# A hybrid decoder layer on one core: ten pairs begun ahead instead of six and eight, HGRN results one head later

## The chip, the cores and the metric

The kernel runs on one core of a Trainium2 chip. The time is the device time of one execution, in microseconds (us); the figure compared is the median of several executions. Engines are called by the profile's names: PE (TensorE's matmuls) and PEld (its weight loads), DVE (VectorE), ACT (ScalarE), POOL (GpSimd) and SP (SyncE, which here only issues transfers; all loads and stores stand in its one queue, in program order).

## The reference

One post-norm decoder layer in f32, on 1024 tokens of width 1024, cut here to what is computed:

```python
z = h @ W_in                      # cut into HGRN q, f, i, g; SWA q, k, v; memory q; three gates
o_a = hgrn2(q, f, i, lb)          # 8 heads, state 128x128, chunks of 64:
                                  #   S_t = diag(f_t) S_{t-1} + (1-f_t) v_t^T ;  o_t = S_t^T q_t
o_a = o_a * rsqrt(mean(o_a^2)) * hg_norm_gain * silu(g)
o_b = sliding_window_attention(...)  # 16 heads, window 128, T5 bias, sinks
o_c = memory_attention(...)          # 4 heads, 256 memory rows
merged = sum_b sigmoid(gate_b) * (o_b @ W_branch_b)
h = layer_norm(alpha * h + merged @ W_out)
h = layer_norm(alpha * h + relu(h @ W_up)^2 @ W_down)
```

## The kernel before, in words

Every f32 operand is held as a rounded high part and the rest (`split`: ACT writes the high part, DVE or POOL subtracts it to get the low part), and a product takes three matmuls: high by high, high by low, low by high. The six large products (gates with the HGRN output gate, three branch products, up, down) are also done by a two-by-two scheme with seven block products instead of eight. The scheme needs sums of quarters of the weights (line 301, on DVE, in place in the raw tile `R`) and of the operand (`combine`). A block product `prod` is twelve matmuls of 128x512.

One *run* makes four 128x512 results from two raw weight tiles: products 1 and 2 need the plain weights `w1` and the left operand `x` (tile `X`); products 3 to 7 need weight sums (`w2`, `w3`, `w4`) and operand sums `xs[3]` to `xs[7]`, which live in tiles `O`, `O`, `T`, `MG`, `BT`. `prepare` loads and sums a run's weights, `run` does the products. Products 1 and 2 of a run need no sums, so some runs begin ahead with a *pair* (`two`, 24 matmuls): the first product is copied to a tile, stored to memory, and read back at the run itself, which then is shorter ("held" below). The pairs stand where the operand sums are still being made:

- Gate stage: six pairs (`EARLY_Z`), and after each of the first four one `x_rest(k)`: two raw tiles of x are loaded, four sums made in place on DVE, five operands split (DVE, ACT, POOL). Then 16 runs.
- Up stage: eight pairs (`EARLY`, in `first_two`), and after each of the first four a deferred `flip_h1(1, n, ...)`: eight transposes of 128x128 on PE, ACT copies, the same sums. Then 16 runs.
- Branch stage: three branches in the order 1, 2, 0, each with three pairs and four runs. After each product result `b_emit` adds the snapshot of another product, multiplies with the gate (`th`, read from memory) and adds to the merged sum. The snapshot sits in a `G` tile, the value `v` goes into the second half of an `S` tile, and the merged sum, where it comes from memory, into a `G` tile.

The HGRN heads run per half of the tokens (`hf`), head by head: `z_q` (query product), `mid` (transposed keys `kt`, masked scores `at`, new state), `outp` (output, its squares, the scaled output `os`), `last` (transposes `os`, multiplies with the output gate `sg`, stores). `kt` and `os` are the halves of one `S` tile. The w_out stage holds eight weight tiles; each result row block does two halves `f` of 24 matmuls over `k`, half 0 first.

A scheduler keeps each engine's program order as written and lets tiles of a name go round in a fixed number of buffers: X 2, O 2, MG 2, BT 2, T 4, W 4, R 4, S 2, G 4; PSUM banks z 3, s 3, t 2. A new tile waits until the one that many turns before it is read for the last time; a load waits in SP's queue, and what stands behind it waits too.

Of the kernel before, what the change touches and what calls it, by code (L numbers as in the profile page):

```python
# [15 lines left out]
P = 128  # L16
# [3 lines left out]
TH = 512  # L20
# [7 lines left out]
NFF = 4096 // 256  # L28
EARLY = 8
EARLY_Z = 6  # L30
EARLY_B = 3
# [5 lines left out]
def hybrid_layer(ctx: ExitStack, tc: tile.TileContext, a: dict, out: bass.AP):  # L37
# [370 lines left out]

    for i in range(EARLY_Z):
        two(zsrc(i)[0], z_keep(i), z_first(i))  # L410
        if i < 4:
            x_rest(i)
    for i in range(16):
# [3 lines left out]
    def zload(br, m, hf):  # L417
        t = st("G", [P, TH])
        nc.sync.dma_start(t, d_z[4 * br + m // 2, 2 * hf + m % 2])
        return t  # L420
# [85 lines left out]
    def swa_phase(hf, x, one, fill_last):  # L506
# [46 lines left out]
        for tp in range(4):  # L553
            if tp < 3:
                qn = st("T", [P, 2, 2, TH], F32R)
                fill = [lambda: z_sq(qn, tp + 1, 0), lambda: one(2 * tp), lambda: z_sq(qn, tp + 1, 1),
                        lambda: one(2 * tp + 1)]
            else:
                fill = [lambda: one(6), lambda: one(7)] + fill_last
            for n in range(4):  # L560
                u = 4 * tp + n
                box = units[u - 1][4] if n % 2 else []
                sc, fl, pv = swa_unit(hf, tp, n, q, kk, bt, pxa[:, n % 2], box)
                units.append((tp, n, fl, pv, box))
                sc()
                fill[n]()
                if u:
                    units[u - 1][2]()
                if u > 1:
                    finish_unit(u - 2)  # L570
            if tp < 3:
                q = qn
# [88 lines left out]
    def hg_head(hf, h, fk, gg, el, x, v, wk):  # L661
# [5 lines left out]
        box = {}  # L667
# [8 lines left out]
        def mid():  # L676
            two_ = st("S", [P, 2, TH])
            kt, box["os"] = two_[:, 0], two_[:, 1]
            box["sg"] = zload(3, h, hf)
            ko = pt("t")  # L680
# [4 lines left out]
            for n in range(4):  # L685
                cs = slice(n * P, (n + 1) * P)
                mm(ao[:, cs], km[:, cs], qm[:, cs], True, True)
            nc.vector.copy_predicated(at, causal.bitcast(I32).unsqueeze(1).broadcast_to([P, 4, P]),
                                      ao.rearrange("p (n c) -> p n c", n=4))
            ko = pt("s")  # L690
            for n in range(4):
# [15 lines left out]
        def outp():  # L707
            osv = box["os"].rearrange("p (n d) -> p n d", d=P)
            oo = pt("s")
            for n in range(4):  # L710
# [19 lines left out]

        return z_q, mid, outp, last

# [16 lines left out]
    for hf in range(NH):  # L749
# [38 lines left out]
        heads = []  # L788
# [10 lines left out]
        for h in range(8):  # L799
            if h == 2:  # L800
                vs.append(st("T", [P, 2, 4, 256]))
                ggs.append(hgs[1][3]())
            if h < 7:
                head(h + 1)
            if h:
                heads[h - 1][2]()
            if h % 2 == 0 and h < 6:
                g = h // 2 + 1
                zv(vs[g // 2][:, g % 2], g)
            heads[h][1]()  # L810
            if h:
                heads[h - 1][3]()
            if hf:
# [12 lines left out]
        if hf == 0:  # L826
            x = nx
        heads[7][2]()
        heads[7][3]()

    accs = {}
# [22 lines left out]
    def b_emit(e, i):  # L854
        br = order[e]

        def emit(b, o, s_):
            t = st("S", [P, 2, TH])
            th, v = t[:, 0], t[:, 1]
            nc.sync.dma_start(th, d_z[4 * br + i, b])  # L860
            home = accs.get((i, b))
            if home is None and e:
                mg = st("G", [P, TH])
                nc.sync.dma_start(mg, d_mg[slot[i, b]])
# [60 lines left out]
    wo = []  # L925
    for i, tag in enumerate(("W", "MG", "MG", "BT", "BT", "W", "T", "T")):
        t = st(tag, [P, 2, 1024], F32R)
        load_here(t[:, 0:1, :], t[:, 1:2, :], a["w_o"][(i % 2) * 4 + i // 2].unsqueeze(1), lo_engine())
        wo.append(t)
    wo = [wo[0::2], wo[1::2]]  # L930
    xv = a["x"].rearrange("(b p) d -> p b d", p=P)
# [80 lines left out]

    for i in range(EARLY):
        first_two(i)
        if i < 4:
            deferred.pop(0)()
# [319 lines left out]
```

## Time and profile before

| | before |
|---|---|
| median of 3 runs | 2241.71 us (2240.56 to 2247.29) |
| profiled execution | 2244.91 us |
| its span in the trace | 2242.9 us |
| PE busy | 2067.9 us, 92% of the span |
| DVE busy | 1415.4 us, 63% |
| ACT busy | 890.2 us, 40% |
| POOL busy | 941.3 us, 42% |
| mean granted TensorE clock | 0.963 of full |

The span is what the trace covers, the profiled execution's time has 2.0 us around it. PE is busy nearly throughout; what it loses is 175 us of the span and some time at a lower granted clock. The stages in order of time: memory keys and values to 56 us; gate stage 56 to 395 (its pairs to 110); window attention and memory heads for the first half of the tokens, HGRN heads 654 to 760; the same for the second half, HGRN heads 1023 to 1145; branches 1132 to 1443; w_out and the first layer norm 1444 to 1549; up pairs 1549 to 1623 and up runs to 1889; down and the last layer norm to 2243.

### The profile page before, as it was taken

Reading aid. Unit: us, or ns where it says so; the run is one execution under the profiler, and the core shown is the slowest. Engines: PE = TensorE matmul, PEld = TensorE weight load, DVE = VectorE, ACT = ScalarE, POOL = GpSimd, SP = SyncE. Lnnn points to the kernel's source line nnn. Section 1 sums busy time; section 2 is a strip of 40 time slices with the busy share of each in tenths; the row PEclk is TensorE's granted clock in tenths of the full one; section 3 lists DMA queues with packets and bytes.
Section 4 is the critical chain, followed back from the end, with each engine's and each line's share of the span. In section 5 each row is a group of like instructions: output and inputs, shape, how many; then the busy total and the mean of one; then the engine's idle time right before and its main releaser. Section 6 shows DMA issues by size and latency. Waiting matters only on the chain.

```text
span 2242.9 us, 27033 instructions
## 1 busy us (share of the span) xinstructions
PE 2067.9 (92%) x9906; PEld 1684.5 (75%) x9906; DVE 1415.4 (63%) x2206; ACT 890.2 (40%) x1558; POOL 941.3 (42%) x430
## 2 busy tenths in 40 slices
PE   8799999999999999999978797898899999999987
PEld 8577888777788777778866575677678887788865
DVE  5643335676554577576475777846566555688898
ACT  4423433444443344363332333413534555433321
POOL 1533333211222222523256454634523334777774
PEclk9899999999999999999999898999899999999998
DMA  8544324322333323554356646434656445744322
GB/s 283 188 154 124 110 97 135 108 86 76 104 118 132 99 95 108 193 202 168 105 191 236 210 151 198 145 112 165 197 186 212 155 155 202 286 154 156 113 85 75
DMA packets 150901, 340.22 MB, mean 152 GB/s; under 512 B 13376, under 2 KB 30960, under 8 KB 150768
## 3 DMA queue, kind: packets, MB, share of 16 engines
q1 hardware_dynamic: 150160, 336.37, 45.1%
q10 hardware_dynamic: 608, 2.11, 0.2%
q8 instruction: 78, 1.28, 0.2%
q14 instruction: 55, 0.45, 0.1%
HBM read 248.76 MB, written 89.67 MB: 151 GB/s over the span
## 4 chain that ended last, share of the span: by engine, by line
PE 33%; DVE 10%; POOL 8%; issue 6%; DMA 6%; ACT 3%; SPq 0%; POOLq 0%; DVEq 0%; ACTq 0%
PE pz L62 16%; PE ps L62 10%; PE pt L62 7%; POOL W L78 3%; DVE S L301 1%; POOL MG L78 1%; DMA R<-d_o 1%; DVE S L870 1%; DVE T L301 1%; DVE R L301 1%; ACT W L77 1%; DMA S<-d_z 1%; POOL BT L78 1%; DMA R<-in_w_up_dram 1%; ACT S L475 1%
## 5 line engine op out<-in xcount | busy, mean ns | idle before, releaser
L78 POOL TENSOR_TENSOR W<-R,W 128x1024 fp32r<-128x1024 f32 x200 | 495.4, 2478 | 959.5 <-ACT W L77 924.8
L77 ACT CAST W<-R 128x1024 fp32r<-128x1024 f32 (+1 forms) x289 | 283.6, 982 | 389.1 <-DVE R L301 168.4
L62 PE MATMUL pz<-X,W 128*128 128x512 f32 x1344 | 342.9, 407 | 33.2 <-POOL W L78 18.1
L62 PEld LDWEIGHTS pz<-X,W 128*128 128x128 f32 x1344 | 256.9, 195 | 95.6 <-POOL W L78 23.9
L62 PE MATMUL pt<-O,W 128*128 128x512 f32 x1056 | 275.3, 410 | 37.8 <-DVE S L301 23.1
L62 PEld LDWEIGHTS pt<-O,W 128*128 128x128 f32 x1056 | 205.3, 197 | 95.4 <-DVE S L301 27.4
L301 DVE TENSOR_TENSOR R<-R,R 128x512 f32<-128x512 f32 x132 | 99.4, 756 | 162.8 <-POOL W L78 138.2
L62 PE MATMUL pz<-O,W 128*128 128x512 f32 x816 | 200.4, 399 | 0.7 <-POOL W L78 0.7
L62 PEld LDWEIGHTS pz<-O,W 128*128 128x128 f32 x816 | 151.7, 190 | 33.3 <-POOL W L78 1.1
L62 PE MATMUL pz<-MG,W 128*128 128x512 f32 x528 | 133.1, 399 | 7.8 <-ACT W L77 7.6
L62 PE MATMUL pz<-BT,W 128*128 128x512 f32 x528 | 131.6, 399 | 8.2 <-DVE G L301 8.2
L62 PE MATMUL ps<-X,W 128*128 128x512 f32 x528 | 131.3, 397 | 0.0
L62 PE MATMUL ps<-T,W 128*128 128x512 f32 x528 | 128.3, 390 | 0.3 <-ACT T L77 0.3
L62 PEld LDWEIGHTS pz<-BT,W 128*128 128x128 f32 x528 | 100.4, 192 | 33.6 <-ACT W L77 8.6
L62 PEld LDWEIGHTS pz<-MG,W 128*128 128x128 f32 x528 | 101.6, 193 | 31.7 <-ACT W L77 9.2
L62 PEld LDWEIGHTS ps<-X,W 128*128 128x128 f32 x528 | 102.1, 194 | 22.1
L62 PEld LDWEIGHTS ps<-T,W 128*128 128x128 f32 x528 | 99.3, 188 | 21.6 <-ACT T L77 0.8
L78 DVE TENSOR_TENSOR W<-R,W 128x512 fp32r<-128x512 f32 (+1 forms) x91 | 92.7, 1019 | 29.2 <-ACT W L77 28.3
L78 POOL TENSOR_TENSOR MG<-R,MG 128x1024 fp32r<-128x1024 f32 (+1 forms) x39 | 100.6, 2580 | 17.7 <-ACT MG L77 16.1
L78 POOL TENSOR_TENSOR BT<-R,BT 128x1024 fp32r<-128x1024 f32 x31 | 84.9, 2740 | 52.8 <-ACT BT L77 52.8
L297 ACT COPY G<-pz 128x512 f32<-128x512 f32 x104 | 60.6, 583 | 96.3 <-PE pz L62 95.3
L301 DVE TENSOR_TENSOR T<-pt,G 128x512 f32<-128x512 f32 x64 | 44.0, 688 | 60.4 <-PE pt L62 56.1
(298 smaller groups left out, 3709.4 us busy)
## 6 DMA issues: line engine op xcount, KB each, us to landing
R<-d_ff SPq DMA_DIRECT2D x49, 512.0 KB, 3.6
R<-in_w_up_dram SPq DMA_DIRECT2D x40, 512.0 KB, 4.1
R<-in_w_b_dram SPq DMA_DIRECT2D x33, 512.0 KB, 4.2
R<-in_w_gate_dram SPq DMA_DIRECT2D x30, 512.0 KB, 4.0
d_z<-T SPq DMA_DIRECT2D x58, 256.0 KB, 2.5
d_ff<-T SPq DMA_DIRECT2D x58, 256.0 KB, 2.8
R<-d_o SPq DMA_DIRECT2D x26, 512.0 KB, 4.0
d_o<-G SPq DMA_DIRECT2D x48, 256.0 KB, 2.3
```

What stands on the lines that cost most here:

```text
L62: nc.tensor.matmul(o, lhsT=l, rhs=r, start=start, stop=stop, skip_group_check=more)
L77: (hi_copy or nc.scalar.copy)(hi, src)
L78: (lo_eng or nc.gpsimd).tensor_tensor(out=lo, in0=src, in1=f32(hi), op=ALU.subtract)
L297: nc.scalar.copy(t, o)
L301: nc.vector.tensor_tensor(out=o, in0=a_, in1=b_, op=op)
L475: nc.scalar.activation(pr[:, j, :], pr[:, j, :], AF.Exp, bias=mx[:, j:j + 1], accum_out=sm_[:, j:j + 1])
L870: nc.vector.scalar_tensor_tensor(out=th, in0=th, scalar=1.0, in1=v, op0=ALU.add, op1=ALU.mult)
```

## The change

- Ten pairs are begun ahead in the gate stage (six before) and ten in the up stage (eight before). One `x_rest`, or one deferred `flip_h1`, stands after every second of the first eight pairs; before it was after each of the first four.
- In the HGRN heads `mid` ends after the mask; the state products are `mid_b`. A head's step is now: `outp` of the head before, `mid` of this head, `last` of the head two before, value product, `mid_b`, query product of the next head. The output gate is loaded in `outp`.
- In `b_emit` the value `v` is written over the snapshot tile (a new `G` tile only for the result without one to spare), and the merged sum is loaded into the second half of the `S` tile.
- The eight w_out weight tiles take other buffers, with half 0 in the first four.
- In the last round of a window-attention half the two fillers that come from the next stage stand ahead of `one(6)` and `one(7)`.

```diff
-EARLY = 8
-EARLY_Z = 6
+EARLY = 10
+EARLY_Z = 10
...
     for i in range(EARLY_Z):
         two(zsrc(i)[0], z_keep(i), z_first(i))
-        if i < 4:
-            x_rest(i)
+        if i % 2 and i < 8:
+            x_rest(i // 2)
...
-                fill = [lambda: one(6), lambda: one(7)] + fill_last
+                fill = fill_last + [lambda: one(6), lambda: one(7)]
...
         def mid():
             two_ = st("S", [P, 2, TH])
             kt, box["os"] = two_[:, 0], two_[:, 1]
-            box["sg"] = zload(3, h, hf)
...
+            box["kt"] = kt
+
+        def mid_b():
+            kt = box["kt"]
             ko = pt("s")
             for n in range(4):
                 mm(ko[:, n * P:(n + 1) * P], kt[:, n * P:(n + 1) * P], v[:, n, vs], True, True)
...
         def outp():
             osv = box["os"].rearrange("p (n d) -> p n d", d=P)
+            box["sg"] = zload(3, h, hf)
...
-            if h < 7:
-                head(h + 1)
             if h:
-                heads[h - 1][2]()
+                heads[h - 1][3]()
+            heads[h][1]()
+            if h > 1:
+                heads[h - 2][4]()
             if h % 2 == 0 and h < 6:
                 g = h // 2 + 1
                 zv(vs[g // 2][:, g % 2], g)
-            heads[h][1]()
-            if h:
-                heads[h - 1][3]()
+            heads[h][2]()
+            if h < 7:
+                head(h + 1)
...
-        heads[7][2]()
         heads[7][3]()
+        heads[6][4]()
+        heads[7][4]()
...
         def emit(b, o, s_):
             t = st("S", [P, 2, TH])
-            th, v = t[:, 0], t[:, 1]
+            th, mg = t[:, 0], t[:, 1]
+            v = st("G", [P, TH]) if b == 3 else s_
             nc.sync.dma_start(th, d_z[4 * br + i, b])
             home = accs.get((i, b))
             if home is None and e:
-                mg = st("G", [P, TH])
                 nc.sync.dma_start(mg, d_mg[slot[i, b]])
             add(v, o, s_)
...
-    for i, tag in enumerate(("W", "MG", "MG", "BT", "BT", "W", "T", "T")):
+    for i, tag in enumerate(("W", "MG", "MG", "BT", "BT", "T", "T", "W")):
         t = st(tag, [P, 2, 1024], F32R)
-        load_here(t[:, 0:1, :], t[:, 1:2, :], a["w_o"][(i % 2) * 4 + i // 2].unsqueeze(1), lo_engine())
+        load_here(t[:, 0:1, :], t[:, 1:2, :], a["w_o"][i].unsqueeze(1), lo_engine())
         wo.append(t)
-    wo = [wo[0::2], wo[1::2]]
+    wo = [wo[0:4], wo[4:8]]
...
     for i in range(EARLY):
         first_two(i)
-        if i < 4:
+        if i % 2 and i < 8:
             deferred.pop(0)()
```

SP's queue at the start of the gate stage, where the pairs' raw weights (`in_w_gate`) and the raw x tiles of `x_rest` (`in_xT`) are asked for, before:

```order
L310 DMA R_647<-in_w_gate_dram 128x1024
L223 DMA R_685<-in_xT_dram 128x2x512
L258 DMA d_mkv<-S_372 128x1024
L223 DMA R_687<-in_xT_dram 128x2x512
L310 DMA R_703<-in_w_gate_dram 128x1024
L223 DMA R_741<-in_xT_dram 128x2x512
L223 DMA R_743<-in_xT_dram 128x2x512
L310 DMA R_759<-in_w_gate_dram 128x1024
L223 DMA R_797<-in_xT_dram 128x2x512
```

and after:

```order
L310 DMA R_647<-in_w_gate_dram 128x1024
L310 DMA R_685<-in_w_gate_dram 128x1024
L258 DMA d_mkv<-S_372 128x1024
L223 DMA R_723<-in_xT_dram 128x2x512
L223 DMA R_725<-in_xT_dram 128x2x512
L310 DMA R_741<-in_w_gate_dram 128x1024
L310 DMA R_779<-in_w_gate_dram 128x1024
L223 DMA R_817<-in_xT_dram 128x2x512
L223 DMA R_819<-in_xT_dram 128x2x512
```

Two weight tiles now stand ahead of each two x tiles, so that four loads fill the four buffers of `R` in one round: an x tile takes the buffer of the x tile one sum before it.

PE in an odd HGRN head of the first half of the tokens (`ps<-T,con` and `ps<-BT` are `outp`, line 682 or 681 the transposes of the keys, `ps<-BT,MG` the scores, `ps<-T,S` the state products of `kt`, line 725 or 729 the transposes of `os`, `pz` the query product), before:

```order
L62 MATMUL ps_5402<-T_4705,con 128x128 x4
L62 MATMUL ps_5402<-BT_5060 128x128 x3
L682 MATMUL pt_5428<-cst,MG_2825 128x128 x4
L62 MATMUL ps_5434<-BT_5060,MG_2825 128x128 x4
L62 MATMUL pz_5468<-X_109,W_5465 128x512
L62 MATMUL pz_5468<-X_110,W_5465 128x512
L62 MATMUL ps_5440<-T_4705,S_5425 128x128 x4
L62 MATMUL pz_5468<-X_109,W_5465 128x512 x2
L62 MATMUL pz_5468<-X_110,W_5465 128x512
L62 MATMUL pz_5468<-X_109,W_5465 128x512
L725 MATMUL pt_5454<-cst,S_5331 128x128 x4
```

and after:

```order
L62 MATMUL ps_5388<-T_4733,con 128x128 x4
L62 MATMUL ps_5388<-BT_5138 128x128 x3
L681 MATMUL pt_5412<-cst,MG_2853 128x128 x4
L62 MATMUL ps_5418<-BT_5138,MG_2853 128x128 x4
L729 MATMUL pt_5424<-cst,S_5111 128x128 x4
L62 MATMUL pz_5451<-X_109,W_5448 128x512
L62 MATMUL pz_5451<-X_110,W_5448 128x512
L62 MATMUL pz_5451<-X_109,W_5448 128x512 x2
L62 MATMUL ps_5431<-T_4733,S_5411 128x128 x4
```

The transposes of `os` are now those of the head before the one whose output was just made, and they stand ahead of the state products; the `S` tile of this head, 5411, takes the buffer that the transposed one, 5111, gives up, because `S` has two.

SP's queue at the start of the up stage (`d_h` is the store of normalised rows, `d_h1t` the left operand of a flip, `d_p` and `d_ff` the store of a pair's first product and result), before:

```order
L310 DMA R_11790<-in_w_up_dram 128x1024
L945 DMA R_11829<-d_h1t 128x8x128
L982 DMA d_h_77<-T_11622 128x1024
L1005 DMA d_p_79<-G_11808 128x512
L982 DMA d_h_77<-T_11622 128x1024
L310 DMA R_11858<-in_w_up_dram 128x1024
L1011 DMA d_ff<-G_11824 128x512
L945 DMA R_11897<-d_h1t 128x8x128
L1025 DMA T_12218<-d_ff 128x512
L310 DMA R_11926<-in_w_up_dram 128x1024
```

and after:

```order
L310 DMA R_11824<-in_w_up_dram 128x1024
L310 DMA R_11863<-in_w_up_dram 128x1024
L951 DMA R_11902<-d_h1t 128x8x128
L988 DMA d_h_77<-T_11656 128x1024
L1011 DMA d_p_79<-G_11842 128x512
L988 DMA d_h_77<-T_11656 128x1024
L1017 DMA d_ff<-G_11858 128x512
L1011 DMA d_p_79<-G_11881 128x512
L310 DMA R_11931<-in_w_up_dram 128x1024
L310 DMA R_11970<-in_w_up_dram 128x1024
L1017 DMA d_ff<-G_11897 128x512
L951 DMA R_12009<-d_h1t 128x8x128
```

The second pair's weights are now asked for ahead of the first flip's left operand; the third pair's stand behind the store of the second pair's first product.

## Rows read from the trace of the kernel before

**Rows 1.** Page, part 1, the whole span: engine busy us (share) xinstructions

```profile
PE 2067.9 (92%) x9906; PEld 1684.5 (75%) x9906; DVE 1415.4 (63%) x2206; ACT 890.2 (40%) x1558; POOL 941.3 (42%) x430
```

**Rows 2.** Windows by stage: from:to length, each engine's busy us (x), PEclk, DMA share, GB/s

```profile
56.40:109.70 53.30, 41.28 (x146) 31.23 (x144) 35.63 (x38) 22.85 (x38) 28.25 (x14) 0.84 0.57 190
...
125.70:394.70 269.00, 265.94 (x1158) 216.01 (x1157) 114.57 (x153) 101.83 (x143) 98.30 (x41) 1.00 0.39 123
...
1549.30:1622.80 73.50, 58.71 (x226) 45.27 (x226) 49.08 (x57) 39.01 (x62) 41.17 (x21) 0.84 0.55 176
```

**Rows 3.** Timeline of PE, gate start: start, us, engine line op out<-in xcount [idle before <-releaser]

```profile
56.44 2.91 PE L62 MATMUL pz<-X,W 128*128 128x512 f32 x12
59.18 2.88 PE L62 MATMUL ps<-X,W 128*128 128x512 f32 x12
...
109.74 3.29 PE L62 MATMUL pz<-MG,W 128*128 128x512 f32 x12 [0.32 <-ACT W L77]
...
125.68 0.62 PE L62 MATMUL pt<-O,W 128*128 128x512 f32 x2
```

**Rows 4.** Timeline of DVE, gate start, third operand sum and what follows

```profile
76.82 0.69 DVE L203 TENSOR_TENSOR R<-R,R 128x512 f32<-128x512 f32 x1 [1.83 <-DMA R<-in_xT_dram]
...
81.71 2.26 DVE L78 TENSOR_TENSOR BT<-R,BT 128x512 fp32r<-128x512 f32 x1
83.89 1.78 DVE L78 TENSOR_TENSOR T<-R,T 128x512 fp32r<-128x512 f32 x1
88.98 0.69 DVE L203 TENSOR_TENSOR R<-R,R 128x512 f32<-128x512 f32 x1 [3.32 <-DMA R<-in_xT_dram]
...
103.27 0.69 DVE L301 TENSOR_TENSOR R<-R,R 128x512 f32<-128x512 f32 x1 [6.15 <-DMA R<-in_w_gate_dram]
```

**Rows 5.** Timeline of POOL, the same stretch

```profile
80.87 2.54 POOL L78 TENSOR_TENSOR W<-R,W 128x1024 fp32r<-128x1024 f32 x1 [0.96 <-ACT W L77]
```

**Rows 6.** DMA issues of the whole span: queue, count, KB each, median us to landing

```profile
R<-in_w_up_dram SPq DMA_DIRECT2D x40, 512.0 KB, 4.1
...
S<-d_z SPq DMA_DIRECT2D x48, 256.0 KB, 3.4
...
R<-in_xT_dram SPq DMA_DIRECT2D x16, 512.0 KB, 5.1
```

**Rows 7.** Timeline of PE, up start

```profile
1549.34 0.61 PE L62 MATMUL pz<-X,W 128*128 128x512 f32 x2
...
1558.75 1.03 PE L951 MATMUL pt<-cst,T 128*128 128x128 f32 x8
...
1564.63 1.22 PE L62 MATMUL pz<-X,W 128*128 128x512 f32 x2 [2.89 <-ACT W L77]
...
1622.78 2.88 PE L62 MATMUL pz<-MG,W 128*128 128x512 f32 x12
```

**Rows 8.** Waits of PE by releaser, whole span: us in total, times, longest

```profile
PE pt L62 <- DVE S L301: 23.1, 9, 7.2
...
PE pt L725 <- DVE S L719: 11.2, 8, 3.5
PE pz L62 <- DVE T L78: 10.8, 2, 10.1
...
PE ps L62 <- ACT S L683: 5.2, 2, 3.3
...
PE ps L62 <- DVE BT L705: 3.4, 2, 2.2
PE pt L487 <- DVE S L480: 3.2, 1, 3.2
```

**Rows 9.** Timeline of DVE, first run of the branch stage

```profile
1163.39 3.41 DVE L301 TENSOR_TENSOR R<-R,R 128x512 f32<-128x512 f32 x2 [4.18 <-POOL W L78]
```

**Rows 10.** Timeline of DVE, before the first w_out rows

```profile
1457.29 2.82 DVE L78 TENSOR_TENSOR X<-S,X 128x512 fp32r<-128x512 f32 x1
1460.03 1.21 DVE L78 TENSOR_TENSOR T<-R,T 128x1024 fp32r<-128x1024 f32 x1
```

More of the change, by code (lines that the diff above doesn't have):

```diff
@@ L729, in last @@
             out_rows(0, h, 1, hf, sg.unsqueeze(1))
-        return z_q, mid, outp, last
+        return z_q, mid, mid_b, outp, last
     outv = out.rearrange("(b p) d -> b p d", p=P)
```

## The prediction, made before the changed kernel was timed

> **What bounds the kernel now.** I read the page first: PE is busy for 2067.9 us of the span [rows 1], so that at most 175 us can be won without removing matmuls, and the change removes none. Then the windows, by stage. The held runs of the gate stage show how it should look, PE busy 265.94 of 269.00 at clock 1.00; the two starts in which pairs are begun ahead do not, 41.28 of 53.30 and 58.71 of 73.50, both at 0.84 [rows 2]. Then PE's timeline in the starts, for what the loss is there. One product of twelve matmuls takes 59.18 - 56.44 = 2.72 us at the full clock, a pair 5.44 [rows 3]. From 56.44 to 109.74 stand six pairs, 32.6 us of work in 53.3: 20.7 are lost before the first held run, and a little more in it. From 1549.34 to 1622.78 stand eight pairs (43.5) and four flips with eight transposes of 1.03 (4.1) in 73.44: 25.8 are lost [rows 7]. Last the waits of PE, for the other edits: those on `os` (11.2), `kt` (5.2), the masked scores or the state (3.4) in the HGRN heads, 10.8 on a T tile in w_out, 23.1 on snapshot arithmetic in the branches, 3.2 in the window attention [rows 8].
>
> **Who is late in the starts.** The starts are not short of weights alone. An operand sum is a chain on DVE that stops between its steps: the third one goes from 76.82 to 83.89 + 1.78 = 85.67, 8.85 us, and the fourth could begin only at 88.98, when its raw tile had come [rows 4]. The first run's weight sums follow at 103.27 and the run at 109.74, 6.47 later [rows 3, 4]. Six pairs cannot cover that; so pairs and sums interleave, and each pair's weights wait in turn.
>
> **A, gate start: +11 (0 to 20.7).** Ten pairs are 54.4 us, to 110.8 if PE never waits. With two pairs to each sum, R's four buffers give a sum the tile of the sum before it, so that its load (5.1 [rows 6]) begins when the chain before has ended: a period of 8.85 + 5.1 = 13.95. The first chain starts at about 56.4, the fourth ends at 56.4 + 3 x 13.95 + 8.85 = 107.1. The first run's raw weights then load (4.1 as for the other weights [rows 6]) and take the 6.47 above: the first held run starts at 117.7. Before, PE had at 109.74 done six pairs; with four more at full speed it would be at 131.5. That is 13.8 sooner. I take 3 off for DVE steps which the extra weight splits on POOL lengthen (the low part in `BT` took 2.26 beside POOL's weight split of 2.54, 80.87 to 83.41, against 0.69 for steps of this size elsewhere [rows 4, 5]). The upper bound is 131.5 - 110.8; the lower is nothing, which comes out if sums still bind and the pairs wait as before.
>
> The Trainium skill ("GPSIMD Engine Reference", section "Specifications") says that POOL shares its SBUF interfaces with VectorE and contends with its instructions that have two SBUF inputs; the stretched step agrees. It speaks against this part of the change: each sum now meets two weight splits of POOL and not one. The rule gives no size.
>
> **G, up start: +7 (0 to 21.8).** The same in the up stage. What remains lost after: the first pair's weights as now, 1558.75 - 1549.34 - 5.44 = 3.97 [rows 7]. The third pair's weights stand in SP's queue behind the store of the second pair's first product, which PE ends at 1558.75 + 2.72 = 1561.5; with 1 for snapshot and issue (chosen), 4.1 for the load [rows 6], 0.96 and 2.54 for the two parts [rows 5] they are ready at 1570.1, where the pair is due at 1564.2: 5.9. Then the sums: four chains, the first after the second pair at about 1565, end at 1565 + 3 x 13.95 + 8.85 = 1615.7, with 4.1 + 6.47 the first run is ready at 1626.3; PE is due at 1549.3 + 54.4 + 4.1 + 3.97 + 5.9 = 1617.7: 8.6. Left lost are 18.5 of 25.8. The upper bound is all but the first pair's wait; the lower, sums that bind as before.
>
> **D, HGRN heads: +10 (0 to 19.8).** The three waits are 11.2 + 5.2 + 3.4 = 19.8 [rows 8]. The order now puts a whole head between `outp` and the transposes of `os`, and a value product and transposes between `kt`'s copy and its use. Two things stay: the last heads of each half have nothing behind them, 2 x 3.5, the longest of the first wait, is 7. And `S` has two buffers, so the copy of `kt` waits until the transposes two heads before are through, which are issued just ahead; I take 3 for it, near the longest wait on `kt`, 3.3. Loading `sg` in `outp` is hidden by the head that lies between it and its use.
>
> **F, w_out: +3 (0 to 8).** PE waited 10.8 in all for T's low part, most of it once, 10.1 [rows 8]. DVE wrote it at 1460.03 for 1.21, behind the last merged operand, X, at 1457.29 for 2.82 [rows 10]. With half 0 in tiles without T, PE goes on through k = 0 to 6, but k = 7 needs that X. What is certainly saved is T's 1.21 and its place; X may come one step (2.82) earlier, when fewer low parts stand ahead. I take 3.
>
> **E and C, branch results and window fillers: +2 each (-3 to 7; -1 to 3.2).** The waits on snapshot arithmetic are 23.1 in nine, the longest 7.2 [rows 8]. But the one place that I followed shows DVE itself stopped: it waits 4.18 for POOL's low part of a weight and then takes 3.41 for two sums [rows 9], ahead of the results in its queue. The edit frees `G` and `S` tiles and takes nothing out of that queue, so most of the 23.1 stays. Of the fillers, the wait is 3.2 once [rows 8]; 2 is taken of it.
>
> **Sum.** 11 + 7 + 10 + 3 + 2 + 2 = 35 on the profiled execution's 2244.9 gives 2209.9. That execution lay 3.2 above the median of the runs, 2241.7; so **2207**.
>
> **Rivals.**
> *Sums still bind (17 in 100).* If each chain is 1.5 us longer for the second POOL split, four chains make 6 in each start, and the first run comes 6 later in A and in G; A + G fall from 18 to 8 with the 3 already taken counted half: about 2217. For it speaks the stretched step; against it that DVE was idle 3.32 ahead of the next sum [rows 4], which is room.
> *S binds in the HGRN heads (8 in 100).* With the transposes, `kt`'s copy and its use in one line of dependence, each of fourteen heads waits 0.7 (half of what the mean of the `os` waits, 11.2 / 8 = 1.4, is): D is 0 and the time about 2217. For it: two buffers; against: the transposes are issued ahead of a product.
> *The clock stays low in the starts (6 in 100).* The starts ran at a granted 0.84, a mix of 2.4 GHz and 1.2 GHz, the held runs at 1.00 [rows 2]; the waits lay between short bursts. If ten pairs with shorter but more numerous waits still run so, then with 0.84 over 54.4 us the pairs take 10 more in A alone; half of A + G is lost: 2216. The Trainium skill ("TensorE: Matmul & The Clock Gate", section "HAM oscillation — how this bites in real kernels") tells of a kernel whose every burst between waits started at the slow clock; by that rule this rival would be likelier than I make it, and the 0.84 agrees.
> *Slower: results hold the G tiles (6 in 100).* `v` now sits in the snapshot tile until the gate has come and the product is done. Four results go through two `S` tiles: two rounds of a load, 3.4 [rows 6], and two DVE steps of 1.7 (half of 3.41 [rows 9]) make 13.6 us. A run's last three products cover 3 x 2.72 = 8.2. Beyond that the next run's snapshot waits for a `G` tile on ACT, and PE's accumulating product for the snapshot: 5.4 at each of the eleven passages between the twelve branch runs, 59 us: about 2268. It decides when the result's last step ends more than 8.2 after the run's end. Against it: loads are asked for when a tile is free, ahead of the results, so the rounds overlap.
> *No change (5 in 100).* The starts give nothing, and what D gives, E takes.
>
> **How the numbers follow.** The forecast has the remaining 58 in 100, with its own range 2193 to 2221 (14 on either side, the size of A's and G's uncertainty together). The range 2178 to 2230 takes in the three rivals near 2217 and the upper bounds of A and D, and leaves out most of no change and the slower case. 0.3% is 6.7 us, about what a measurement of this kernel can tell from no change. Faster by more: the forecast and the three rivals, less their tails, 0.87; within: 0.06; slower: 0.07.
>
> **What the profile after would show.** Right: ten pairs from 56.4 with waits of a few us in all and the first held run near 118; the same in the up stage, with one wait near 6 at the third pair; the waits on `os` below 7 in all; DVE's idle times between sums bounded by `in_xT` loads; w_out's wait near 7 on X. Wrong: DVE or POOL unbroken through the starts and PE waiting on them; waits of PE on `kt` in every head; waits of ACT for `G` tiles in the branches. A stage that the change doesn't touch and that moves by more than 5 us would upset the sum too.

## The result and the profile after

The changed kernel's median is 2230.7 us (2223.48 to 2233.29, six runs) against 2244.47 for the kernel before (six runs, 2240.56 to 2248.89); the ratio is 0.9935, 95% interval 0.9915 to 0.9955. Run once more, beside the experiments, it was 2224.1 (2220.99 to 2231.73) against 2243.8, ratio 0.9919 (0.9899 to 0.9938). So it is 14 to 20 us faster, where 35 were forecast; the first median lies just outside the forecast's range (2178 to 2230), the second inside it, and the gain is 0.4 to 0.6 of the forecast one. That the second lies inside is luck, because errors of opposite sign stand against each other: by the table below A and D gave 18 us less than forecast, E gave 9 more.

The page of the changed kernel, engines' busy times; they answer to [rows 1], and hardly differ: the 16 us came out of PE's idle time and clock.

```profile
PE 2061.4 (93%) x9906; PEld 1681.2 (76%) x9906; DVE 1418.6 (64%) x2218; ACT 883.7 (40%) x1546; POOL 938.2 (42%) x430
```

The windows of its starts and of its held gate runs, as in [rows 2] (columns as there):

```profile
56.20:122.10 65.90, 58.84 (x243) 46.55 (x241) 38.64 (x41) 29.07 (x45) 36.44 (x17) 0.95 0.61 204
145.80:393.90 248.10, 243.59 (x1057) 197.07 (x1057) 115.60 (x156) 87.94 (x122) 88.68 (x37) 1.00 0.42 133
1536.90:1617.50 80.60, 67.35 (x274) 52.16 (x273) 49.78 (x57) 42.41 (x69) 44.34 (x22) 0.89 0.54 183
```

The clock in the two starts rose from 0.84 to 0.95 and 0.89, but see what the ten pairs are followed by. PE's timeline of the gate start, answering to [rows 3]:

```profile
56.18 2.91 PE L62 MATMUL pz<-X,W 128*128 128x512 f32 x12
...
87.39 3.02 PE L62 MATMUL ps<-X,W 128*128 128x512 f32 x12 [0.97 <-DVE G L301]
92.99 5.49 PE L62 MATMUL pz<-X,W 128*128 128x512 f32 x12 [2.58 <-ACT G L297]
...
105.69 3.01 PE L62 MATMUL ps<-X,W 128*128 128x512 f32 x12 [1.32 <-DVE G L301]
110.83 3.04 PE L62 MATMUL pz<-X,W 128*128 128x512 f32 x12 [2.12 <-ACT G L297]
...
122.10 0.73 PE L62 MATMUL pz<-MG,W 128*128 128x512 f32 x2
...
137.40 5.46 PE L62 MATMUL pz<-BT,W 128*128 128x512 f32 x12 [7.72 <-DVE G L301]
142.66 3.35 PE L62 MATMUL ps<-T,W 128*128 128x512 f32 x12
145.84 2.88 PE L62 MATMUL pt<-O,W 128*128 128x512 f32 x12
```

PE goes through five and a half pairs almost without a wait (56.18 to 87.39 holds 31.2 us, eleven products at 2.72 are 29.9). Then it waits on results that ACT and DVE have not taken out of PSUM, 0.97, 2.58, 1.32 and 2.12, and the first held run begins at 122.10, 4.4 later than forecast, but 9.1 sooner than before when four more pairs are counted (109.74 + 21.76, less 0.26 for the earlier start). The run itself then waits 7.72 before its third product, which runs near half clock (142.66 - 137.40 = 5.26 for twelve matmuls). Its last product starts at 145.84; before, that was 125.68 [rows 3], with the four pairs 147.44. Of 9.1 us won, 1.3 are left there, and none at the stage's end, where nine held runs have waited 0.37 each for their sums and five did before (the next stage begins at 410.24, before at 409.89).

The up start, answering to [rows 7]:

```profile
1536.95 0.61 PE L62 MATMUL pz<-X,W 128*128 128x512 f32 x2
...
1546.61 2.91 PE L62 MATMUL pz<-X,W 128*128 128x512 f32 x12
...
1552.08 1.03 PE L957 MATMUL pt<-cst,T 128*128 128x128 f32 x8
...
1557.57 1.22 PE L62 MATMUL pz<-X,W 128*128 128x512 f32 x2 [2.50 <-ACT W L77]
...
1566.34 2.88 PE L62 MATMUL pz<-X,W 128*128 128x512 f32 x12
...
1582.96 1.03 PE L957 MATMUL pt<-cst,T 128*128 128x128 f32 x8
...
1588.32 1.22 PE L62 MATMUL pz<-X,W 128*128 128x512 f32 x2 [2.37 <-ACT W L77]
...
1617.47 4.82 PE L62 MATMUL pz<-MG,W 128*128 128x512 f32 x12 [3.45 <-ACT W L77]
```

Ten pairs and the flips' 4.1 fill 58.5 of the 80.5 us to the first held run; 22.0 are lost where 25.8 were. The flips stand two at a time, after the second pair and after the sixth. (The sentence ahead of the prediction that the scheduler keeps each engine's order as written is not right: it moves work across such places, here whole flips.)

PE's waits over the whole span, answering to [rows 8]:

```profile
PE pt L62 <- DVE G L301: 22.4, 9, 6.3
...
PE pt L729 <- DVE S L723: 9.1, 3, 5.4
...
PE ps L62 <- DVE BT L672: 3.4, 2, 2.5
PE ps L62 <- DVE con L687: 3.1, 1, 3.1
...
PE ps L62 <- DVE T L78: 2.8, 1, 2.8
...
PE pz L62 <- ACT X L77: 2.1, 1, 2.1
PE pt L681 <- DVE MG L674: 2.1, 1, 2.1
PE pz L62 <- DVE X L78: 2.0, 1, 2.0
...
PE ps L62 <- ACT S L682: 1.6, 1, 1.6
...
PE pz L62 <- DVE T L78: 0.7, 1, 0.7
```

The wait on T's low part fell from 10.1 to 2.8 in w_out, where it now comes in half 1 (row `ps`); the 0.7 of row `pz` lies at 6 us, in both kernels. Those on `os` fell from 11.2 to 9.1 only, in three places and not eight, those on `kt` from 5.2 to 1.6; and new ones stand beside them: on the first head's keys (line 674, 2.1), on query products (line 672, 3.4 in two heads), on the last head's masked scores (`con`, 3.1).

### The profile page after: what moved, and what is told of

Its sections match the earlier page's. It is cut to its first block, busy times and chain, and to the rows that moved or that the text cites. A ratio compares the mean times of both kernels' runs of the same rounds, so it can differ in the third digit from the quotient of the medians.

```text
span 2226.6 us, 27069 instructions
## 1 busy us (share of the span) xinstructions
PE 2061.4 (93%) x9906; PEld 1681.2 (76%) x9906; DVE 1418.6 (64%) x2218; ACT 883.7 (40%) x1546; POOL 938.2 (42%) x430
## 4 chain that ended last, share of the span: by engine, by line
PE 40%; DVE 7%; POOL 6%; DMA 5%; issue 5%; ACT 2%; SPq 0%; POOLq 0%; DVEq 0%; ACTq 0%
PE pz L62 20%; PE ps L62 12%; PE pt L62 7%; POOL W L78 2%; DMA R<-d_o 1%; DMA R<-in_w_up_dram 1%; DVE R L301 1%; DMA R<-in_w_b_dram 1%; DVE S L876 1%; DVE T L301 1%; POOL BT L78 1%; ACT W L77 1%; DVE G L301 1%; DMA S<-d_z 1%; POOL MG L78 0%
## 5 line engine op out<-in xcount | busy, mean ns | idle before, releaser
L62 PE MATMUL pz<-X,W 128*128 128x512 f32 x1344 | 338.2, 404 | 15.8 <-POOL W L78 5.6
L62 PE MATMUL pt<-O,W 128*128 128x512 f32 x1056 | 273.9, 409 | 36.4 <-DVE G L301 22.4
L62 PE MATMUL pz<-BT,W 128*128 128x512 f32 x528 | 131.5, 398 | 14.0 <-DVE G L301 13.6
L297 ACT COPY G<-pz 128x512 f32<-128x512 f32 x92 | 53.4, 581 | 78.1 <-PE pz L62 78.1
```

Of the source, the lines that this page charges most:

```text
L62: nc.tensor.matmul(o, lhsT=l, rhs=r, start=start, stop=stop, skip_group_check=more)
L297: nc.scalar.copy(t, o)
```

## Stage by stage

Twenty kernels were profiled, most of which share most stages. So each stage has repeats, and they say how far one profiled execution can be trusted: the same code gave 350 to 354 in the gate stage and 279 to 287 in the branches. Below, each stage is PE's first instruction in it to PE's first in the next, in us, with the mean and the lowest and highest over the kernels that have the old or the new code there. "Gate" has ten pairs and two to a sum as new; the new code of F leaves out the two kernels whose branch results are the old ones (45.7 and 45.8).

| stage (term) | old code | new code | won | forecast |
|---|---|---|---|---|
| gate (A) | 352.4 (348.5 to 355.3), 3 | 351.4 (350.3 to 354.1), 6 | 1.0 | 11 |
| window attention, both halves (C) | 155.7 and 163.3, 2 | 156.0 and 161.3 (160.9 to 164.5), 18 | 1.7 | 2 |
| memory and HGRN heads, both halves (D) | 206.6 and 217.2, 3 | 206.0 and 216.2, 17 | 1.6 | 10 |
| branches (E) | 294.3 (292.5 to 296.2), 4 | 283.0 (278.6 to 287.4), 16 | 11.3 | 2 |
| w_out to the fourth row block (F) | 47.7 (47.7 to 47.8), 2 | 43.8 (42.5 to 44.2), 16 | 3.9 | 3 |
| up (G) | 343.6 (343.5 to 343.7), 2 | 341.0 (338.9 to 342.3), 17 | 2.6 | 7 |

The gains of the table add to 22, near the 22.5 by which the second profile of the changed kernel is shorter than the first of before (2242.9 - 2220.4), and above the 14 and 20 of the medians. Half of the gain is in the one place where almost none was forecast.

## The experiments

Each kernel is the changed one with the edit shown, unless the text says otherwise; ratios are to the kernel before on the same chip.

**The gate start as before.**

```diff
-EARLY_Z = 10
+EARLY_Z = 6
...
-        if i % 2 and i < 8:
-            x_rest(i // 2)
+        if i < 4:
+            x_rest(i)
```

> The changed kernel with the gate start of before (six pairs, one operand sum after each of the first four). Theory: the ten pairs win about 9 us up to the first held run and give all of it back in the first held run, whose sums and read-back snapshots stand behind the pairs' results on ACT, DVE and SP, so this kernel takes as long as the changed one, 2231 within 4, and the window attention begins within 1 us of 394 as there. Rival, the prediction's own term: the gate start is worth 11, so this kernel takes about 2241.

Measured: 2224.0 (2218.32 to 2230.52), ratio 0.9912 (0.9886 to 0.9938), the same as with the ten pairs. Term A is worth nothing that can be told from zero, by intervals of some 6 us on either side.

**Ten pairs, one sum after each of the first four.** Only the second half of that edit.

> The changed kernel with ten pairs, but one operand sum after each of the first four pairs as before. It parts the number of pairs from their interleaving. Theory: waits of the first four pairs as before (some 16 us), but six pairs behind the last sum cover the first held run's preparation, so that the run's own waits go; gate stage 0 to 4 us shorter than in the changed kernel, 2227 to 2231. Rival: two pairs per sum are what wins and the first held run is slow whatever covers it; then the gate stage is 9 longer than in the changed kernel, 2240.

Measured: 2222.3 (2217.94 to 2224.65), ratio 0.9897 (0.988 to 0.9913). Its first held run begins at 128.75, 6.6 later than in the changed kernel, waits 1.58 and no more, and the gate stage is 349.8 (350.1 in the mean of three kernels with this order): not longer for all its waits at the first pairs. A later start of the held runs cost nothing, so something other than that start sets their pace.

**Twelve pairs.** `EARLY_Z = 12`.

> The changed kernel with twelve pairs at the gate and not ten. Theory: the first held run's wait for its weight sums (7.7 us and some half clock) is a fixed time after the last operand sum, and two more pairs (10.9 us) cover it: gate stage about 8 shorter, 2223. Rival: the sums stand behind the pairs' results in ACT's and DVE's order and move with them, so the wait stays and each held run more costs its 0.4: 2231 to 2232.

Measured: 2231.8 (2228.03 to 2233.83), ratio 0.9944 (0.9929 to 0.9959); the gate stage 350.6. The wait is still 6.04. The rival held in the gate stage: the run's preparation moves with the pairs. That the time is the rival's too is luck: it is 8 and 10 above the two runs before it here, and none of that lies in the gate stage (350.6 against 351.4 in the table).

**The HGRN order of before in the changed kernel, and the new order alone in the kernel before.** The edit is the part of the diff on `hg_head` and the loop over heads, taken out or put in.

> The changed kernel with the HGRN head order of before. Theory: as the stages read, the new order won 1.3 in the first half of the tokens and nothing in the second, since the waits of the last heads grew: this kernel takes 1 to 3 longer, 2232 to 2234. Rival, the prediction's term: it is worth 10, 2241.

> The kernel before with the new HGRN head order alone. Theory: the order is worth nothing, since the waits that go at the middle heads come back at the first and last ones: within 3 of before, both HGRN stretches within 1 of before. Rival, the prediction: 10 faster. Second rival, taken from the run without the order: it costs 9, by what follows it in the branch stage.

Measured: 2221.0 (2218.84 to 2224.33), ratio 0.9899 (0.9884 to 0.9913) without it; alone 2245.4 (2236.37 to 2249.91), ratio 1.0004 (0.999 to 1.0019). The order alone is worth nothing within 0.2%. The first of these runs suggested that it costs 9; the second rival fell with the run alone and with the changed kernel's repeat:

> The changed kernel unaltered, as the measure for the runs beside it on the same chip: 2223 to 2233 as before. Gate stage 351 to 354, branch stage 281 to 287: the same code gave these spreads in the runs that kept these parts.

Measured: 2224.1, as above, gate 351.4, branches 283.4.

**The branch results of before.** The edit is the part of the diff in `b_emit`, taken out.

> The changed kernel with the branch results of before (value in the S tile, merged sum in a G tile). Theory: the stages read 6 to 12 for this edit, against 2 in the prediction, because the addition then waits for an S tile with the gate's load and holds DVE: branch stage back to about 292, the time 8 above the unaltered kernel. Rival, the prediction's 2: 2 above it.

**The value in the snapshot tile, but the merged sum in a G tile.**

```diff
-            th, mg = t[:, 0], t[:, 1]
+            th = t[:, 0]
             v = st("G", [P, TH]) if b == 3 else s_
...
             if home is None and e:
+                mg = st("G", [P, TH])
                 nc.sync.dma_start(mg, d_mg[slot[i, b]])
```

> The changed kernel, but the merged sum is again loaded into a G tile; the value stays in the snapshot tile. Theory: what wins in the branches is that the merged sum's load no longer takes one of the four G tiles, for which the next snapshot on ACT, and PE behind it, waited at the ends of the second and third branch; then this kernel's branch stage is 290 to 294, as with all of the old results, and its time 2235 to 2240. Rival: the value wins, which needs no S tile any more before it can be added: branch stage 280 to 287, 2224 to 2230.

Measured: 2238.3 (2233.59 to 2244.2), ratio 0.9974 (0.9961 to 0.9986), and 2237.4 (2228.61 to 2242.86), ratio 0.9969 (0.9954 to 0.9985); branch stages 292.5 and 296.2. So this edit holds about 12 of the gain, and it comes from the merged sum's load leaving the G tiles. Writing the value to the snapshot tile without that wins nothing that the two runs show (though it takes a G tile more for one result in four), and the mechanism in the first of these two expectations (the addition waiting for an S tile) is wrong. In the kernel with the old results, at the end of the second branch, ACT and PE:

```profile
1329.91 1.04 ACT L77 CAST MG<-R 128x1024 fp32r<-128x1024 f32 x1 [2.96 <-DMA R<-d_c]
1330.86 0.58 ACT L297 COPY G<-pz 128x512 f32<-128x512 f32 x1
```

```profile
1332.22 4.62 PE L62 MATMUL pt<-O,W 128*128 128x512 f32 x12 [2.82 <-DVE S L301]
1336.68 2.90 PE L62 MATMUL pz<-X,W 128*128 128x512 f32 x12
```

and the same place in the changed kernel's repeat:

```profile
1324.98 1.05 ACT L77 CAST W<-R 128x1024 fp32r<-128x1024 f32 x1 [3.30 <-DMA R<-in_w_b_dram]
1325.94 0.58 ACT L297 COPY G<-pz 128x512 f32<-128x512 f32 x1
```

```profile
1328.21 2.88 PE L62 MATMUL pt<-O,W 128*128 128x512 f32 x12
```

Two merged sums hold G tiles from 1327.8 on (the loads stand in SP's queue there). The snapshot, for which DVE's addition and behind it PE's accumulating product wait, stands on ACT behind a split that waits 2.96 for its operand; in the other kernel it stands one place further up, right behind the weight's split, and is done 4.9 sooner in a kernel that is 1.0 ahead there (the product before it starts at 1326.51 and 1325.49). The product waits 2.82 and then takes 1336.68 - 1332.22 = 4.46 in the one, and waits not at all in the other. That the snapshot stands further back for want of a G tile is read from the two orders and the two edits; no row shows ACT waiting for one here.

**Both fastest parts.** The old HGRN order and one sum after each of the first four of ten pairs.

> The changed kernel with the old HGRN order and with one operand sum after each of the first four of its ten pairs. Theory: both are gains beside the changed kernel, and they add: 4 at the gate, the rest by the order: about 2217, the fastest so far. Rival: the run without the new order was fast by chance; then about 2224.

Measured: 2221.8 (2217.69 to 2225.73), ratio 0.9904 (0.9887 to 0.9922): faster than before, not told apart from the changed kernel.

**A flip after each of the first four up pairs, with ten pairs.**

```diff
-        if i % 2 and i < 8:
+        if i < 4:
             deferred.pop(0)()
```

> The changed kernel with ten pairs in the up stage, and a flip after each of the first four as before. Theory: as at the gate, what counts is how much pair work lies behind the last sum: the four flips cost what they cost before, six pairs behind them cover the first run, and up start to down takes 338 to 340 as in the changed kernel, or less. Rival: fewer waits because of two pairs to a flip; then 343 as before.

Measured: 2231.2 (2230.11 to 2237.58), ratio 0.9948 (0.9928 to 0.9968); up start to down 348.0, longer than with eight pairs (343.6). Neither the theory nor the rival had that. In the up stage two pairs to a flip is what wins, and ten pairs with the old places lose 4; the theory from the gate does not carry over.

**What holds the first held gate run.** Eight kernels. Weight sums of the first two held runs on POOL, then of the first four:

```diff
-    def prepare(src0, src1, first):
+    def prepare(src0, src1, first, eng=None):
+        def add(o, a_, b_, op=ALU.add):
+            (eng or nc.vector).tensor_tensor(out=o, in0=a_, in1=b_, op=op)
...
-        ws = prepare(*zsrc(i), i >= EARLY_Z)
+        ws = prepare(*zsrc(i), i >= EARLY_Z, nc.gpsimd if i < 2 else None)
```

> The changed kernel with the weight sums of the first two held gate runs made on POOL and not on DVE. Theory: the first held run waits 6 to 8 us because these sums wait on DVE for their raw weights, with the last pairs' results and the run's own addition queued behind them; off DVE, the results come at once, the run's wait falls below 4, and the gate stage is 3 to 6 shorter, 346 to 349. Rival: the raw weights themselves come late, for want of a buffer in R; then the wait stays above 6 and the stage at 351 to 354.

> The changed kernel with the weight sums of the first four held gate runs on POOL. With two, the third run's sums took the place ahead of the first run's addition on DVE (133.53 and 134.82 there, behind a wait for raw weights of 2.06). Theory: DVE's order is the cause, and with four nothing stands ahead; the first held run then waits only for its snapshot to be read back, below 5, and the gate stage is 348 to 350. Rival: the wait stays above 6, and it is the snapshot's way to memory and back.

The pairs' second results in S tiles (`z_first`: `t = st("S", [P, 2, TH])[:, 0]`), alone, with the same in the up pairs, with one sum after each of the first four, and with four runs' sums on POOL:

> The changed kernel with a gate pair's second result in an S tile, which nothing else uses there, and not in a G tile. Theory: G's four tiles are what holds the first held run: each pair takes two until their stores have landed, the snapshot that is read back needs one more, and the last pairs' results wait for one; then its wait of 6 to 8 us falls below 4 and the gate stage is 3 to 6 shorter, 346 to 349. Rival: the raw weights of the second run come late whatever G does; then the wait stays above 6 and the stage at 351 to 354.

> The same, and the up pairs' second result in an S tile too. Theory: the up start waits for weights behind the flips and not for G, so up start to down stays at 339 to 342 and the time is that of the run with the gate alone within 2. Rival: G binds there too; then 335 to 338.

> The same with one operand sum after each of the first four gate pairs. Theory: with G relieved the wait that this order avoided is gone, and what is left is its waits for weights at the first pairs: gate stage not shorter than with two pairs to a sum, 347 to 352. Rival: the two gains add, 344 to 346.

> The same with the pairs' second results in S tiles. Theory: the snapshot is read back some 2 sooner when its G tile comes free sooner, so the wait falls below 3 and the gate stage to 346 to 349; neither edit alone shows the whole. Rival: no shorter than with either alone, 351 to 354.

The snapshots read back into S tiles, asked for ahead of the run's weights, alone and with four runs' sums on POOL:

```diff
-            t = st("G", [P, TH])
+            t = st("S", [P, 2, TH])[:, 0]
             nc.sync.dma_start(t, d_g1[i])
...
+        p1 = z_p1(i)() if i < EARLY_Z else None
         ws = prepare(*zsrc(i), i >= EARLY_Z)
-        run(ws, z_p1(i)() if i < EARLY_Z else None, None, z_emit(i))
+        run(ws, p1, None, z_emit(i))
```

> The changed kernel with the first held runs' snapshots read back into S tiles, asked for ahead of the runs' weights; the first two are then read back in the middle of the pairs. Theory: the first held run's addition has two conditions that end within 2 us of each other, the next run's weight sums ahead of it on DVE and the snapshot's way back; with the second alone removed the first still holds it: the wait is 6 to 8, the gate stage 350 to 354. Rival: the read-back alone is the cause: wait below 3, stage 344 to 348.

> The same, and the weight sums of the first four held runs on POOL. Theory: with both conditions removed the wait is below 2 and the gate stage 344 to 348, 4 to 6 below the changed kernel. Rival: a third condition, the weights of the run's own product on POOL, keeps it above 4, stage 350 or more.

| kernel | median us (ratio) | wait of the first held run's third product | gate stage |
|---|---|---|---|
| changed | 2230.7 (0.9935), 2224.1 (0.9919) | 7.72 | 354.1, 351.4 |
| two runs' sums on POOL | 2224.0 (0.9905) | 6.50 | 351.8 |
| four runs' sums on POOL | 2225.0 (0.9917) | 6.99 | 352.9 |
| results in S | 2222.2 (0.9911) | 8.01 | 352.2 |
| the same, up too | 2225.4 (0.9926) | 8.02 | 351.9 |
| the same, a sum after each of the first four | 2220.3 (0.9905) | 1.58 | 351.4 |
| results in S, four runs' sums on POOL | 2227.3 (0.9936) | 6.56 | 349.9 |
| read-back early | 2222.7 (0.9901) | 5.67 | 347.9 |
| read-back early, four runs' sums on POOL | 2225.3 (0.9916) | 0.57, then 6.82 two products on | 348.4 |

(The third product, `pz<-BT,W`, adds to the bank that the first has filled, so it waits until DVE's addition of the snapshot has read that bank.) With results in S nothing changed, so G's tiles alone are not the cause here. The up pairs' results in S changed nothing either (341.6). Each of the other edits alone uncovers the next condition. With the early read-back the gate stage (347.9, 348.4) is some 2 us below the lowest of the six repeats of the unaltered one (350.3), one execution each; the old code spread over 348.5 to 355.3, and no median shows the 2 us. With four runs' sums off DVE, DVE's row for the run's addition shows it waiting for the snapshot's way back:

```profile
137.68 0.69 DVE L301 TENSOR_TENSOR G<-pz,G 128x512 f32<-128x512 f32 x1 [4.56 <-DMA G<-d_g]
```

With the read-back early, the addition (131.58) stands behind the weight sums of the third run and then of the second, and the third run's sums wait for raw weights:

```profile
128.84 0.69 DVE L301 TENSOR_TENSOR R<-R,R 128x512 f32<-128x512 f32 x1 [3.20 <-DMA R<-in_w_gate_dram]
...
131.58 0.68 DVE L301 TENSOR_TENSOR G<-pz,S 128x512 f32<-128x512 f32 x1
```

With both removed the product starts at once, and the next but one waits 6.82: the DVE step that frees its bank stands behind a low part that waits 10.09 for its high part, which waits for a sum on POOL, and POOL had waited 5.06 for the same raw weights.

```profile
127.33 2.99 PE L62 MATMUL pz<-BT,W 128*128 128x512 f32 x12 [0.57 <-DVE G L301]
...
139.86 4.52 PE L62 MATMUL pt<-O,W 128*128 128x512 f32 x12 [6.82 <-DVE T L301]
```

```profile
137.28 1.20 DVE L78 TENSOR_TENSOR W<-R,W 128x512 fp32r<-128x512 f32 x1 [10.09 <-ACT W L77]
...
139.12 0.69 DVE L301 TENSOR_TENSOR T<-pt,G 128x512 f32<-128x512 f32 x1
```

```profile
130.29 1.29 POOL L330 TENSOR_TENSOR R<-R,R 128x512 f32<-128x512 f32 x1 [5.06 <-DMA R<-in_w_gate_dram]
```

The chain is the same in all of them. In the changed kernel POOL, SP and DVE show it from its start:

```profile
125.91 4.73 POOL L78 TENSOR_TENSOR W<-R,W 128x1024 fp32r<-128x1024 f32 x2 [5.30 <-ACT W L77]
```

```profile
128.34 0.33 SPq L310 DMA_DIRECT2D R<-in_w_gate_dram  x1
...
129.81 0.32 SPq L395 DMA_DIRECT2D G<-d_g  x1
```

```profile
133.83 0.69 DVE L301 TENSOR_TENSOR R<-R,R 128x512 f32<-128x512 f32 x1 [3.94 <-DMA R<-in_w_gate_dram]
...
136.57 0.68 DVE L301 TENSOR_TENSOR G<-pz,G 128x512 f32<-128x512 f32 x1
```

R has four tiles. The third run's second raw tile is asked for at 128.34, as the first of POOL's two splits ends (125.91, 4.73 together); 5.5 later it is there (133.83), and the third run's sums, the second run's last sums and the first run's addition (136.57) follow on DVE in that order. The read-back stands behind the request in SP's queue, at 129.81. Pairs take R tiles too, ahead of these, and more pairs push the request back: 126.0 to 128.3 in the six repeats, 135.16 with twelve pairs, so 6.8 to 9.2 later for the 10.9 that two pairs cover. With one sum after each of the first four pairs it is at 127.11, as in the repeats, though the first held run begins 6.6 later. That the request waits for R, and R for POOL's split, is read from the order of these rows in every run; a fifth R tile was not tried, so this cause is argued and not shown.

## Why the prediction was wrong, and where it was right

**A failed at the step "with four more at full speed it would be at 131.5. That is 13.8 sooner".** The chains of sums were sized well at first (starts at 56.56, 70.03, 84.83 and 101.44 on DVE, periods 13.5, 14.8 and 16.6, forecast 13.95), and the first held run came 9.1 sooner for the 10.8 forecast. But the step takes it that the run goes on from there as before. It does not: the weights of the runs go through R, which the pairs use as well, and by the rows come at a time that the pairs push back. What was won ahead of the run was waited for in it, 7.72 before one product, and the kernel with the old gate start takes as long (ratio 0.9912 against 0.9935 and 0.9919). This is close to the rival "sums still bind", with the weights' sums where that rival named the operand's.

**D failed at the step "Two things stay".** They are the tail and `kt`, forecast at 7 + 3 us. The waits of the middle heads did go, but others came, at the first head's keys, at query products, at the last masked scores and at the last heads' `os`: 9.1 + 3.1 + 2.1 + 1.6 + 3.4 = 19.3 after, where the sum allowed 10. Counted alike, over all of PE's waits in the two HGRN stretches, it is 23.4 before, 20.5 after and 17.5 in the changed kernel's repeat. So a few us of waits went, and the stage times show 1.6. In the last heads DVE is late itself, with small operations that lie between transposes:

```profile
1129.64 2.31 DVE L1224 TENSOR_TENSOR sm<-sm 128x4 f32<-128x4 f32 x1 [1.12 <-POOL sm L1223]
1131.98 2.27 DVE L1225 TENSOR_TENSOR sm<-sm,sm 128x4 f32<-128x4 f32 x1
...
1134.68 0.69 DVE L723 TENSOR_TENSOR S<-ps,sm 128x512 f32<-128x512 f32 x1
```

beside POOL's splits of branch operands:

```profile
1129.57 2.35 POOL L78 TENSOR_TENSOR W<-R,W 128x1024 fp32r<-128x1024 f32 x1
1131.89 2.33 POOL L78 TENSOR_TENSOR BT<-R,BT 128x1024 fp32r<-128x1024 f32 x1
```

DVE's two steps of 128x4 last until POOL's instruction ends, 2.31 and 2.27. In the last head of the kernel before, one step met POOL so, and the step that takes 2.31 here takes 0.16 alone:

```profile
1137.42 2.35 DVE L1216 TENSOR_SCALAR sm<-sm 128x4 f32<-128x4 f32 x1
...
1140.89 0.16 DVE L1218 TENSOR_TENSOR sm<-sm 128x4 f32<-128x4 f32 x1 [0.53 <-POOL sm L1217]
```

PE's longest wait on `os`, 5.4 in the rows of the waits, ends with the third of DVE's rows of after; the longest before was 3.5. A price of 7 for the tail was taken from the old order's longest wait, and the tail is where the new order puts its waits.

**E failed at the step "takes nothing out of that queue, so most of the 23.1 stays".** In the first pair of profiles the 23.1 did stay (22.4), but over all of them it fell: 23.1 to 27.3 in the four kernels with the old branch code, 17.7 to 22.5 in the sixteen with the new, means 25.2 and 20.4. All of PE's idle time in the stage fell by 7.1 in the mean (51.6 to 44.5); the other 4.2 of the 11.3 are products that run shorter. What the edit gives is a G tile that snapshots no longer lack, and that was not looked for: 11 for 2. The rival "results hold the G tiles" named the resource and had the sign the wrong way round.

**G was right in kind and too large, 7 for 2.6 (25.8 - 22.0 = 3.8 in the start itself).** The term mis-sized is a second wait behind two flips, which the sum had at nothing. Its terms: the first pair's wait 3.97 forecast, 1546.61 - 1536.95 - 5.44 = 4.2 measured; the third pair's 5.9, measured 1566.34 - 1552.08 - 2.06 - 5.44 = 6.8; the first run's 8.6, measured 3.45; and the seventh pair's, behind the other two flips, which the sum did not have, 1597.15 - 1582.96 - 2.06 - 5.44 = 6.7.

**F and C came out near their forecasts, by stage times alone.** No run takes either edit out, and C's 1.7 is within the spread (160.9 to 164.5 for the new code's second half, 162.6 and 164.1 for the old). F's wait on T fell from 10.1 to 2.8, and the one on X came in its place, 2.1 and 2.0. Of F's 3.9 about 2 need the edit of the branch results too: with the old ones w_out takes 45.7.

**The clock rival fell**: the granted clock in the starts rose with the shorter waits, 0.84 to 0.95 and 0.89. So did the rival that S binds in the HGRN heads: the waits on `kt` went from 5.2 to 1.6. What the Trainium skill tells ("TensorE: Matmul & The Clock Gate", section "HAM oscillation — how this bites in real kernels"), that a burst behind a wait starts at the slow clock, is still seen in single products: those behind waits of 7.72 and 2.82 took 5.26 and 4.46 us for twelve matmuls that take 2.72 at the full clock, the first near the lower of the two levels, the second between them.

## What to carry to other kernels

Work begun ahead may not cover the preparation of what follows where it uses the same buffers: count the tiles of every ring that passes through both, and follow the first request behind the covered stretch, not only the last operand. When a wait is removed and the time stays, remove the next condition too before calling the first harmless; here each removal alone won at most 2.1 of 7.7 us. And look at what an edit gives back in tiles, since a tile in a ring that another engine is short of was worth more here than every reordering.

## What the runs showed that was not expected

A DVE instruction of 128x4 lasted 2.31 us beside a split on POOL, against 0.16 alone: it ended as POOL's ended (1131.95 and 1131.92). The Trainium skill ("GPSIMD Engine Reference", section "Specifications") names the shared SBUF interfaces for instructions with two SBUF inputs; the rows agree, and in them the small step takes as long as is left of POOL's instruction, whatever its own size is. And one profiled execution is no measure of a stage here: the branch stage of the same code took 279 to 287 us, which is more than most of the terms that were to be told apart.
